# A pool of residual buffers with delayed reuse, and two norms moved into the next block, in a two-layer streaming encoder

## The chip, the cores and the metric

One Trainium2 chip, eight cores on two dies (cores 0 to 3 and 4 to 7). Every core runs the same program on two of the 16 sequences; there is no traffic between cores. The metric is the time of the slowest core in microseconds (us), lower is better. The program has two states: in some executions the cores of one die (at times both) are granted a lower TensorE clock, and the time is 1 to 19% longer.

## The reference, cut to what matters

```python
def reference(x, ...):                      # x: (16, 2048, 1024) float32
    h = x
    for layer in range(2):
        h = h + 0.5 * swiglu(rms_norm(h, ffn1_norm[layer]), ...)
        hn = rms_norm(h, mix_norm[layer])
        if layer == 0: h = h + chunked_relpos_attention(hn, ...)   # 16 heads, band of 9 chunks
        else:          h = h + mla_attention(hn, ..., shared k, v) # 8 heads, block-causal
        h = h + 0.5 * swiglu(rms_norm(h, ffn2_norm[layer]), ...)
        if layer == 0: k_nope, k_rope, v = mla_shared_kv(rms_norm(h, kv_norm), ...)
    return rms_norm(h, final_norm)
```

The residual stream `h` of a core (two sequences of 2048 tokens, 1024 channels, float32, 16 MB) does not stay on the core. Each block reads it from HBM, adds its result, and writes it to HBM again.

## The kernel before

The blocks run in the order F00 F01 A0 A1 F10 F11 F20 F21 B0 B1 F30 F31 (F feed-forward, A and B attention; the last digit is the sequence). In each block, TensorE works through 32 output pieces of 128 channels x 512 tokens. A piece ends in one VectorE add: PSUM bank plus residual piece. `Resid` brings the residual piece (256 KB) in, and takes the sum out. All these transfers are issued by SyncE from one queue, in program order:

```python
class Resid:
    def __init__(self, src, srcR, dst, dstR, order, more=(), n_rr=4):
        self.ring = [(r[:], rR, 'r%d' % k) for k, (r, rR) in enumerate(rr[:n_rr])] + list(more)
        ...
    def ahead(self, n=None):                       # issue loads for pieces < n
        n = len(self.ring) - 1 if n is None else n
        while self.n < min(n, len(self.order)):
            i, sb = self.order[self.n]
            r, rR, ch = self.ring[self.n % len(self.ring)]
            dma(r, xview(src, i, sb), [srcR[sb][i]], [rR], ch + 'l')
            self.n += 1
    def add(self, i, sb, po, poR, scale):
        ...
        TT(r, po, r, ALU.add, [poR, rR], [rR])     # bank + residual, in place
        dma(xview(dst, i, sb), r, [rR], [dstR[sb][i]], ch + 's')
        self.ahead(n + len(self.ring))             # loads piece n+9 into the buffer of piece n-1
```

The ring has 10 buffers in A (four `rr`, six in the arena), 7 in B, 4 in F. While a block ends, the norms of the next block run beside it: `norm_plan` spreads, over the projections, per 512-token slice a 2 MB load (`load`), squares on ScalarE (`sq`), a sum over channels on TensorE and the reciprocal root (`st`), and eight VectorE multiplies into `hn` (`nrm`).

```python
# a_block, head: 8 projections before the first scores, on two PSUM banks (MISC_A = [6, 7])
fill = [g for a in range(8) for g in proj(a)]
for _ in range(8):
    fill.pop(0)()
...
# a_block, at the start of the last head pair
if a == 7 and bl == 0:
    more = [...arena buffers at 84, 86, 2, 6, 12, 14 K...]
    rs = Resid(src, srcR, dst, dstR, [(i, t0 + s) for s in range(4) for i in range(8)], more)
    rs.ahead()
    wo = wo_groups('a', ao, aoR, rs, t0)           # 32 output projections of 8 matmuls
```

The softmax here doesn't subtract the row's maximum and nothing guards it: scores larger than these inputs give would overflow.

## Time and profile before

| | before |
|---|---|
| two runs before the prediction | 5358.67 (fast) and 6034.01 (slow), median 5696.34 us |
| profiled run (slow state) | cores 0 to 3: 5328 to 5345 us; cores 4 to 7: 5507 to 5530 us |
| TensorE busy, page of the slowest core | 97% |
| TensorE waits on core 0 | 135 us |

The page's first two sections show a kernel with one full engine. What is left to gain can only be found by asking where that engine stands still:

```profile
PE 5380.4 (97%) x29888; PEld 2603.0 (47%) x29888; DVE 1948.6 (35%) x3083; ACT 1533.0 (28%) x2068; POOL 231.9 (4%) x681
PE   8999999999899999999999999999998999999999
```

Slices of 10 us of core 0 at the end of A0 show the place in one look. The columns are window, length, TensorE busy, granted clock, DMA share, GB/s:

```profile
1300.00:1310.00 10.00, 7.84 (x37) 1.00 0.97 211
1310.00:1320.00 10.00, 0.00 (x0) 0.55 1.03 184
1320.00:1330.00 10.00, 6.29 (x16) 0.60 0.73 227
```

TensorE does nothing for one slice, and its clock falls in that slice and stays low in the next. The names in such lines: `ps` is a PSUM bank; `xs` is the residual stream in HBM; `arena`, `rr`, `sg` and `hn` are buffers on the core; `wbf<-wblob` is the load of a weight tile; SPq is the queue that SyncE issues from. In a line of waits, such as those in the prediction, the three numbers are total us, count and longest us. In a line of the order of time, the bracket is the idle time ahead of the group and what ended it.

### The profile page before, as it was taken

Reading aid. Unit: us, or ns where it says so; the run is one execution under the profiler, and the core shown is the slowest. Engines: PE = TensorE matmul, PEld = TensorE weight load, DVE = VectorE, ACT = ScalarE, POOL = GpSimd, SP = SyncE. Lnnn points to the kernel's source line nnn. Section 1 sums busy time; section 2 is a strip of 40 time slices with the busy share of each in tenths; the row PEclk is TensorE's granted clock in tenths of the full one; section 3 lists DMA queues with packets and bytes.
Section 4 is the critical chain, followed back from the end, with each engine's and each line's share of the span. In section 5 each row is a group of like instructions: output and inputs, shape, how many; then the busy total and the mean of one; then the engine's idle time right before and its main releaser. Section 6 shows DMA issues by size and latency. Waiting matters only on the chain.

```text
span 5530.0 us, 80374 instructions; the slowest of 8 cores (5328.5 to 5530.0 us)
## 1 busy us (share of the span) xinstructions
PE 5380.4 (97%) x29888; PEld 2603.0 (47%) x29888; DVE 1948.6 (35%) x3083; ACT 1533.0 (28%) x2068; POOL 231.9 (4%) x681
## 2 busy tenths in 40 slices
PE   8999999999899999999999999999998999999999
PEld 3444444455455444444444444445654664444445
DVE  2113111346566412321531351143444443133312
ACT  3111111147467412111211211113443442121311
POOL 0000000000010000000000000000000000000000
PEclk7888888899999999999999999999999999999999
DMA  5125312522522622632642363263264255255442
GB/s 132 31 37 146 95 31 35 150 68 68 148 54 70 189 51 51 169 77 41 150 125 39 73 166 75 42 161 85 62 166 107 62 155 137 39 128 151 107 86 92
DMA packets 237403, 532.20 MB, mean 96 GB/s; under 512 B 21472, under 2 KB 30176, under 8 KB 237024
## 3 DMA queue, kind: packets, MB, share of 16 engines
q1 hardware_dynamic: 194544, 356.11, 20.8%
q0 software_dynamic: 42480, 170.97, 18.5%
q8 instruction: 247, 4.05, 0.3%
q14 instruction: 132, 1.08, 0.1%
HBM read 577.88 MB, written 111.67 MB: 125 GB/s over the span
## 4 chain that ended last, share of the span: by engine, by line
PE 90%; DMA 5%; DVE 2%; issue 1%; ACT 1%; SPq 0%; DVEq 0%; POOL 0%; ACTq 0%; POOLq 0%
PE ps L407 90%; DMA xs<-rr 2%; DMA xs<-arena 1%; DVE hn L418 1%; DVE arena L424 1%; DVE arena L414 1%; ACT arena L411 0%; ACT rstd L411 0%; DMA rr<-xs 0%; DMA xn<-xT 0%; PE ps L1476 0%; SPq L404 0%; DMA arena<-xs 0%; ACT L411 0%; DMA xn<-tabT 0%
## 5 line engine op out<-in xcount | busy, mean ns | idle before, releaser
L407 PE MATMUL ps<-hn,wbf 128*128 128x512 bf16 (+1 forms) x13280 | 3050.9, 392 | 43.2 <-DVE arena L414 30.4
L407 PEld LDWEIGHTS ps<-hn,wbf 128*128 128x128 bf16 x13280 | 1324.2, 100 | 1683.0 <-issue 504.5
L407 PE MATMUL ps<-arena,wbf 128*128 128x512 bf16 (+1 forms) x6520 | 1481.5, 388 | 11.7 <-DVE rr L414 5.5
L414 DVE TENSOR_TENSOR arena<-sg,ps 128x512 bf16<-128x512 f32 (+1 forms) x706 | 483.9, 686 | 1961.5 <-PE ps L407 1910.5
L407 PEld LDWEIGHTS ps<-arena,wbf 128*128 128x128 bf16 x6520 | 648.7, 100 | 796.1 <-issue 220.3
L411 ACT ACTIVATE sg<-ps 128x512 f32<-128x512 f32 (+1 forms) x706 | 420.6, 596 | 1990.9 <-PE ps L407 1971.7
L411 ACT ACTIVATE arena<-ps 128x1024 bf16<-128x1024 f32 (+2 forms) x520 | 484.7, 975 | 465.6 <-PE ps L407 429.0
L407 PE MATMUL ps<-arena 64*128 64x256 bf16 (+8 forms) x5728 | 567.8, 264 | 28.9 <-DVE arena L414 6.4
L407 PEld LDWEIGHTS ps<-arena 128*128 128x128 bf16 (+1 forms) x5728 | 348.8, 96 | 253.6 <-issue 174.3
L411 ACT ACTIVATE sq<-xn 128x1024 f32<-128x1024 f32 (+3 forms) x264 | 243.5, 949 | 530.6 <-DVE sq L414 267.4
L418 DVE SCALAR_TENSOR_TENSOR rr<-ps,rr 128x512 f32<-128x512 f32 x224 | 154.9, 691 | 649.2 <-PE ps L407 633.7
L424 DVE CAST arena<-ps 128x512 bf16<-128x512 f32 x368 | 252.0, 689 | 259.6 <-PE ps L407 259.1
L456 POOL DMA_DIRECT2D wbf<-wblob x290 | 153.2, 528 | 4054.9 <-PE ps L407 4003.9
L418 DVE SCALAR_TENSOR_TENSOR hn<-xn,gains_sb,rstd 128x512 bf16<-128x512 f32 (+1 forms) x440 | 295.4, 736 | 62.1 <-ACT rstd L411 62.1
L411 ACT ACT_TABLE_LOAD x45 | 57.7, 1283 | 381.7 <-PE ps L407 380.0
L414 DVE TENSOR_TENSOR sq<-sq 128x1024 f32<-128x1024 f32 (+1 forms) x128 | 139.0, 1086 | 36.6 <-ACT sq L411 33.3
L407 PE MATMUL ps<-wbf,hn 128*128 128x128 bf16 x2048 | 124.9, 219 | 3.0 <-DVE arena L424 3.0
L407 PEld LDWEIGHTS ps<-wbf,hn 128*128 128x128 bf16 x2048 | 118.3, 98 | 17.8 <-issue 8.3
L424 DVE COPY arena<-ps 128x512 f32<-128x512 f32 (+1 forms) x192 | 109.5, 598 | 43.7 <-PE ps L1476 36.2
L414 DVE TENSOR_TENSOR arena<-arena 128x512 bf16<-128x512 bf16 (+1 forms) x304 | 106.6, 372 | 35.8 <-ACT arena L411 27.2
L411 ACT ACTIVATE rstd<-ps,eps_sb 128x512 f32<-128x512 f32 (+1 forms) x74 | 50.0, 676 | 237.0 <-PE ps L407 236.8
L407 PE MATMUL ps<-sq,ones_sb 128*128 128x512 bf16 (+1 forms) x276 | 74.6, 400 | 40.0 <-ACT sq L411 23.3
(51 smaller groups left out, 1254.3 us busy)
## 6 DMA issues: line engine op xcount, KB each, us to landing
wbf<-wblob POOLq DMA_DIRECT2D x192, 512.0 KB, 5.3
xn<-xs SPq DMA_DIRECT2D x48, 2048.0 KB, 13.9
xs<-rr SPq DMA_DIRECT2D x282, 256.0 KB, 3.8
rr<-xs SPq DMA_DIRECT2D x218, 256.0 KB, 4.7
wbf<-wblob POOLq DMA_DIRECT2D x60, 704.0 KB, 7.2
arena<-xs SPq DMA_DIRECT2D x70, 256.0 KB, 4.5
xs<-arena SPq DMA_DIRECT2D x70, 256.0 KB, 4.7
wbf<-wblob POOLq DMA_DIRECT2D x22, 768.0 KB, 7.8
```

The source lines that it names most:

```text
L407: sch.add('pe', lambda e: e.matmul(out, lhsT, rhs, start=start, stop=stop, skip_group_check=skip), rd, wr)
L411: sch.add('act', lambda e: e.activation(out, in_, func, **kw), rd, wr, None, [out], srcs)
L414: sch.add('dve', lambda e: e.tensor_tensor(out, a, b, op), rd, wr, None, [out], [a, b])
L418: sch.add('dve', lambda e: e.scalar_tensor_tensor(out, a, sc, b, op0, op1), rd, wr, None, [out], srcs)
L424: sch.add(eng, lambda e: e.tensor_copy(out, in_), rd, wr, None, [out], [in_])
L456: sch.add('pool', lambda e, wb=wb, w=w, src=src: e.dma_start(out=wb[:, 0:w], in_=src), rd, [wbR], 'wq%d' % k)
```

## The change

The intent is to keep TensorE fed where one block ends and the next begins. The ring becomes a pool of free buffers, in which a buffer is offered again only `cool` adds after its own; more buffers join the pool in A and B; two of A1's four norms move from A0's tail into A1's start; and A's first projections use six PSUM banks.

```diff
+LATE_A = [('A', 0, 1)]
 class Resid:
-            def __init__(self, src, srcR, dst, dstR, order, more=(), n_rr=4):
+            def __init__(self, src, srcR, dst, dstR, order, more=(), n_rr=4, cool=3):
+                self.cool = cool
+                self.hot = []
-                self.ring = [...] + list(more)
+                self.free = list(more) + [(r[:], rR, 'r%d' % k, 99) for k, (r, rR) in enumerate(rr[:n_rr])]
+            def ahead(self):
+                while self.n < len(self.order):
+                    self.free = [f for f in self.free if f[3] >= self.n]   # 'last piece' of a buffer
+                    if not self.free: break
+                    slot = self.used[(i, sb)] = self.free.pop(0)
+                    ...load...
             def add(...):
                 ...add, store...
-                self.ahead(n + len(self.ring))
+                self.hot.append(slot)
+                if len(self.hot) > self.cool:
+                    self.free.append(self.hot.pop(0))
+                self.ahead()
 # feed-forward blocks
+            rs = Resid(..., cool=1)
 # A, last head pair
+                    more = f32_slots(ar, [o_ * K for o_ in (2, 6, 12, 14)], 'rc')
+                    more += [(r[:], rR, 'rs%d' % k, 27) for k, (r, rR) in enumerate(sg)]
+                    more += f32_slots(ar, [84 * K, 86 * K], 'ra')
+                if a == 7 and bl == 2:
+                    free_s = [s for s in (1, 2) if next_jobs[s].fine]
+                    rs.more(f32_slots(hn_ar, [...four per slice in free_s...], 'rh', 23))
 # A, head
+            if late_a: fill[9:15] = fill[12:15] + fill[9:12]
+            cur['misc'] = MISC_E                    # six banks
+            for n in range(8):
+                if late_a and n == 0: jobs[2].st()
+                elif late_a and n == 6: jobs[3].st()
                 fill.pop(0)()
+                if late_a and n < 4: jobs[2].nrm(n); jobs[3].sq(n)
+            cur['misc'] = MISC_A
 # B: three hn buffers more where the next block is F30, and later up to nine more
# [cut: norm_plan(n_full=2) for A1, jobs[3].nrm among A1's first groups, B's pool in full, bookkeeping]
```

More of the change, by code (lines that the diff above doesn't have):

```diff
@@ L618, in nrm, with hn @@
                         ALU.mult, ALU.mult, [self.xR, rsR, gR], [self.hR[0][c] if self.fine else self.oR])
+            def hn(self, c):
+                return self.hR[0][c] if self.fine else self.oR
             def store(self):
@@ L678, in kfin, with norm_plan @@
                     self.xR.rd.extend(r.rd)
-        def norm_plan(jobs, pitch, lag=1, base=0):
+        def norm_plan(jobs, pitch, lag=1, base=0, n_full=4):
             plan = {}
@@ L689, in norm_plan @@
                 kv, final = j.a[4], j.a[5]
-                for q in range(4):
-                    put(b - 4 + q, j.sq, q)
+                if n <= n_full:
+                    for q in range(4):
+                        put(b - 4 + q, j.sq, q)
+                if n >= n_full:
+                    continue
                 put(b, j.st)
@@ L732, in next_plan @@
         def next_plan(blk, next_jobs, par):
-            if BLOCKS[BLOCKS.index(blk) + 1] in LATE:
+            nb = BLOCKS[BLOCKS.index(blk) + 1]
+            if nb in LATE:
                 for n in range(1, 4):
@@ L736, in next_plan @@
                 return late_plan(next_jobs, *par[1])
+            if nb in LATE_A:
+                for n in range(2, 4):
+                    next_jobs[n].fine = True
+                plan = norm_plan(next_jobs, *par[0], n_full=2)
+                return plan
             return norm_plan(next_jobs if blk[0] == 'A' else next_jobs[::-1], *par[0])
         class Resid:
-            def __init__(self, src, srcR, dst, dstR, order, more=(), n_rr=4):
+            def __init__(self, src, srcR, dst, dstR, order, more=(), n_rr=4, cool=3):
+                self.cool = cool
+                self.hot = []
                 self.a = (src, srcR, dst, dstR)
@@ L744, in __init__, with more @@
                 self.n = 0
-                self.ring = [(r[:], rR, 'r%d' % k) for k, (r, rR) in enumerate(rr[:n_rr])] + list(more)
-                self.first = 0
-                self.slots = {}
-            def ahead(self, n=None):
+                self.free = list(more) + [(r[:], rR, 'r%d' % k, 99) for k, (r, rR) in enumerate(rr[:n_rr])]
+                self.used = {}
+            def ahead(self):
                 src, srcR = self.a[:2]
-                n = len(self.ring) - 1 if n is None else n
-                while self.n < min(n, len(self.order)):
+                while self.n < len(self.order):
+                    self.free = [f for f in self.free if f[3] >= self.n]
+                    if not self.free:
+                        break
                     i, sb = self.order[self.n]
-                    r, rR, ch = self.ring[self.n % len(self.ring)]
+                    slot = self.used[(i, sb)] = self.free.pop(0)
+                    r, rR, ch, _ = slot
                     dma(r, xview(src, i, sb), [srcR[sb][i]], [rR], ch + 'l')
                     self.n += 1
+            def more(self, slots):
+                self.free += slots
+                self.ahead()
             def add(self, i, sb, po, poR, scale):
                 dst, dstR = self.a[2:]
-                n = self.order.index((i, sb))
-                r, rR, ch = self.ring[n % len(self.ring)]
+                slot = self.used.pop((i, sb))
+                r, rR, ch, _ = slot
                 if scale == 1.0:
@@ L766, in add, with f32_slots @@
                 dma(xview(dst, i, sb), r, [rR], [dstR[sb][i]], ch + 's')
-                self.ahead(n + len(self.ring))
+                self.hot.append(slot)
+                if len(self.hot) > self.cool:
+                    self.free.append(self.hot.pop(0))
+                self.ahead()
+        def f32_slots(arena, offs, name, last=99):
+            out = []
+            for n, o in enumerate(offs):
+                a_, r_ = arena.take(o, 1024)
+                out.append((a_.bitcast(F32), r_, '%s%d' % (name, n), last))
+            return out
         def ffn_block(blk, jobs, src, srcR, dst, dstR, bg_up, next_jobs, last):
@@ L843, in ffn_block @@
                 late_norms(1)
-            rs = Resid(src, srcR, dst, dstR, [(i, t0 + s) for i in range(8) for s in range(4)])
+            rs = Resid(src, srcR, dst, dstR, [(i, t0 + s) for i in range(8) for s in range(4)], cool=1)
             kv = blk in KV_IN
@@ L1018, in proj @@
                 out = []
+                gv_ = {}
                 for s in range(4):
@@ L1027, in gqk @@
                         w3, wR = w3_()
-                        pp, ppR = misc(MISC_A)
+                        pp, ppR = misc(cur['misc'])
                         for c in range(8):
-                            MM(pp, w3[:, c, o:o + 128], job.o3[:, c, :], c == 0, c == 7, [wR, job.oR], [ppR])
+                            MM(pp, w3[:, c, o:o + 128], job.o3[:, c, :], c == 0, c == 7, [wR, job.hn(c)], [ppR])
                         CP(dst_[0], pp, [ppR], [dst_[1]])
@@ L1034, in gv @@
                         w3, wR = w3_()
-                        pp, ppR = misc(MISC_A)
+                        pp, ppR = misc(cur['misc'])
                         for tt in range(4):
@@ L1038, in gv @@
                                 MM(pp[:, tt * 128:(tt + 1) * 128], job.o3[:, c, tt * 128:(tt + 1) * 128],
-                                   w3[:, c, 256:384], c == 0, c == 7, [wR, job.oR], [ppR])
+                                   w3[:, c, 256:384], c == 0, c == 7, [wR, job.hn(c)], [ppR])
                         CP(v_out(v_[s][0]), pp.rearrange('p (t h n) -> p t h n', t=4, h=2), [ppR], [v_[s][1]])
@@ L1042, in gv, with done @@
                             w_done(('a', 'qkv', a))
-                    out += [lambda s=s, g=gqk: g(0, q_[s]), lambda s=s, g=gqk: g(128, k_[s]), gv]
+                    def done(s=s):
+                        gv_[s]()
+                        made.add((a, s))
+                    gv_[s] = gv
+                    out += [lambda s=s, g=gqk: g(0, q_[s]), lambda s=s, g=gqk: g(128, k_[s]), done]
                 return out
@@ L1068, in scores @@
                 a, QB, rs_, first, last = groups[g]
-                assert len(fill) <= 3 * (31 - 4 * a - QB) or a == 7, (a, QB, len(fill))
+                assert (a, QB) in made, (a, QB)
                 q_, k_, v_ = bufs[a % 2]
@@ L1140, in a_block @@
             bias_load(0)
+            late_a = blk in LATE_A
+            made = set()
             fill = [g for a in range(8) for g in proj(a)]
-            for _ in range(8):
+            if late_a:
+                fill[9:15] = fill[12:15] + fill[9:12]
+            cur['misc'] = MISC_E
+            for n in range(8):
+                if late_a and n == 0:
+                    jobs[2].st()
+                elif late_a and n == 6:
+                    jobs[3].st()
                 fill.pop(0)()
+                if late_a and n < 4:
+                    jobs[2].nrm(n)
+                    jobs[3].sq(n)
+            cur['misc'] = MISC_A
             bias_make(0)
@@ L1156, in a_block @@
             shape(1)
+            if late_a:
+                jobs[3].nrm(0)
             for b in range(NB):
@@ L1166, in a_block @@
                 if a == 7 and bl == 0:
-                    more = []
-                    for i, o in enumerate((84 * K, 86 * K, 2 * K, 6 * K, 12 * K, 14 * K)):
-                        a_, r_ = ar.take(o, 1024)
-                        more.append((a_.bitcast(F32), r_, 'ra%d' % i))
+                    more = f32_slots(ar, [o_ * K for o_ in (2, 6, 12, 14)], 'rc')
+                    more += [(r[:], rR, 'rs%d' % k, 27) for k, (r, rR) in enumerate(sg)]
+                    more += f32_slots(ar, [84 * K, 86 * K], 'ra')
                     rs = Resid(src, srcR, dst, dstR, [(i, t0 + s) for s in range(4) for i in range(8)], more)
@@ L1173, in a_block @@
                     wo = wo_groups('a', ao, aoR, rs, t0)
+                if a == 7 and bl == 2:
+                    assert len(fill) <= 3
+                    free_s = [s for s in (1, 2) if next_jobs[s].fine]
+                    rs.more(f32_slots(hn_ar, [s * 4096 + o_ * 1024 for s in free_s for o_ in range(4)], 'rh', 23))
                 if a == 6:
@@ L1197, in a_block @@
                     shape(2 * b + 3)
+                if late_a and b < 3:
+                    jobs[3].nrm(b + 1)
                 while done < n_fill and fill:
@@ L1242, in kv_home @@
                         v_.rearrange('p (h t n) -> p h t n', h=2, t=4), vR, vo)
-            kvh = [[kv_home() for _ in range(2 if s < 2 else 1)] for s in range(4)]
+            kvh = []
+            for s in range(4):
+                o_kv3 = o
+                kvh.append([kv_home() for _ in range(2 if s < 2 else 1)])
             qh = []
             for s in range(4):
+                o_q3 = o
                 q_, qR = tk(1024)
@@ L1552, in b_block @@
             rs = wo = None
+            got = False
             def do_fill():
@@ L1570, in b_block @@
                 if p == 3 and bl == 0:
-                    more = []
-                    for i in range(4):
-                        a_, r_ = ar.take(o_ckv + i * 1024, 1024)
-                        more.append((a_.bitcast(F32), r_, 'rb%d' % i))
+                    more = f32_slots(ar, [o_ckv + i * 1024 for i in range(4)], 'rb', 27)
+                    if next_jobs[3].fine:
+                        more += f32_slots(hn_ar, [3 * 4096 + i * 1024 for i in range(3)], 'rh', 27)
                     rs = Resid(src, srcR, dst, dstR, [(i, t0 + s) for s in (3, 2, 1, 0) for i in range(8)], more, 3)
@@ L1577, in b_block @@
                     wo = wo_groups('b', ao, aoR, rs, t0, 0)
+                if p == 3 and bl == 8:
+                    assert seen['p'] >= last_unit(3, lambda u: u[1] >= 6)
+                    more = f32_slots(ar, [o_kv3, o_kv3 + 1024, o_q3], 'rk')
+                    if next_jobs[2].fine:
+                        more += f32_slots(hn_ar, [2 * 4096 + i * 1024 for i in range(3)], 'rg', 23)
+                    rs.more(more)
+                if p == 3 and not got and (3, 0) in made:
+                    got = True
+                    end = 99 if seq == 0 else 27
+                    rs.more([(r[:], rR, 'rs%d' % k, end) for k, (r, rR) in enumerate(sg)]
+                            + [(rr[3][0][:], rr[3][1], 'r3', end)])
                 if p == 2 and next_jobs:
```

## The prediction

> **What bounds the kernel now.** I read the list of cores first, because the two times on record (5358.67 and 6034.01 us) are two states of one program, then the page's busy shares, then TensorE's waits, then TensorE and the DMA-issuing queue around the few places where TensorE stands still.
>
> ```profile
> core 0: 5340.0 us, clock 0.990
> core 1: 5345.0 us, clock 0.992
> die 0 (median of its cores): 5341.6 us, clock 0.992
> die 1 (median of its cores): 5516.9 us, clock 0.957
> ```
>
> The page is of a core of the slow die. I work on core 0, of the undisturbed one, and predict the fast state, whose one run took 5358.67 us. The windows of core 0, added up, give PE 5192 us busy in 5345 us: 153 us, 2.9%, is all the idleness there is, and everything that the change does must come out of it. TensorE's waits on core 0, the largest:
>
> ```profile
> PE ps L407 <- DVE arena L414: 44.7, 31, 14.7
> PE ps L407 <- DVE rr L414: 22.9, 7, 11.8
> PE ps L407 <- ACT sq L411: 17.9, 11, 7.9
> ```
>
> L414 is VectorE's add or multiply; with out tile rr or arena it is above all the residual add that empties a PSUM bank of an output projection. Asked by stretch, the waits of the eight feed-forward blocks are almost nil (none at all from 90 to 960 us). The long ones stand at four seams, where an attention block ends: A0 to A1 (about 1308 us), A1 to F10 (1679), B0 to B1 (3977), B1 to F30 (4383). The order-of-time view of TensorE there:
>
> ```profile
> 1295.59 12.25 PE L407 MATMUL ps<-arena,wbf 128*128 128x512 bf16 x56
> 1322.52 6.29 PE L407 MATMUL ps<-hn,wbf 128*128 128x512 bf16 x16 [14.68 <-DVE arena L414]
> 1330.81 3.08 PE L407 MATMUL ps<-wbf,hn 128*128 128x128 bf16 x32 [1.99 <-DVE arena L424]
> ...
> 1690.66 3.57 PE L407 MATMUL ps<-sq,ones_sb 128*128 128x512 bf16 x8 [11.84 <-DVE rr L414]
> ...
> 3978.80 1.89 PE L407 MATMUL ps<-hn,wbf 128*128 128x512 bf16 x8 [1.45 <-DMA wbf<-wblob]
> 3991.97 14.81 PE L407 MATMUL ps<-hn,wbf 128*128 128x512 bf16 x56 [11.29 <-DVE arena L414]
> ...
> 4391.45 3.57 PE L407 MATMUL ps<-hn,wbf 128*128 128x512 bf16 x8 [6.57 <-DVE arena L414]
> 4400.95 3.57 PE L407 MATMUL ps<-sq,ones_sb 128*128 128x512 bf16 x8 [5.92 <-DVE rr L414]
> ```
>
> The first matmul of the next block needs a bank that an unfinished residual add still holds. VectorE in turn waits for data: from 1285 to 1332 us its waits are 21.9 us for arena<-xs and 5.3 us for rr<-xs, the loads of old residual pieces. And those loads are late because of the queue that issues them. From 1270 to 1332 us its waits are these two lines, and its order of time shows one load behind one store:
>
> ```profile
> SPq L152 <- DMA xs<-arena: 20.7, 7, 11.7
> SPq L152 <- DMA xs<-rr: 19.5, 4, 9.2
> ```
> ```profile
> 1300.89 0.74 SPq L404 DMA_DIRECT2D xs<-rr  x1
> 1313.36 0.32 SPq L404 DMA_DIRECT2D arena<-xs  x1
> 1313.78 0.58 SPq L404 DMA_DIRECT2D xs<-rr  x1
> 1323.60 0.32 SPq L404 DMA_DIRECT2D rr<-xs  x1
> ```
>
> So the chain is: store of piece n-1 lands, then the load of piece n+9 into its buffer can be issued, then the queue is free for the next store. TensorE makes a piece in 8 matmuls, 1.73 us; the queue needs a landing, 4.6 or 4.7 us in the median for these stores, up to 12 us late in the tail. Ten buffers (seven in B) are a lead that some 20 fast pieces use up.
>
> **What the Trainium skill says.** "DMA: Bandwidth & Descriptors", section "Anatomy of one DMA": any semaphore wait happens on the issuing sequencer before dispatch, and the completion receipt dominates the fixed cost. The trace agrees: 40.2 us of the queue's time in the two lines above are waits for stores. "TensorE: Matmul & The Clock Gate", section "Part 1: The HAM clock gate": after an idle window of about 3.4 us TensorE runs at half its clock until it has been busy for a window. The trace agrees: after 14.68 us of idleness 16 matmuls took 6.29 us against 3.62 us for such a group when warm. So each seam costs more than its wait. "HBM Reference", section "Specifications (TRN2)": about 358 GB/s per core when the pair is active. From 1185 to 1345 us the hardware queue moved 19.93 MB in 39.5% of 160 us, some 315 GB/s while busy, and no slice stayed above about 400; I use this as the limit that a faster tail could meet.
>
> **The change part by part.**
> (1) The residual ring becomes a pool of free buffers. A buffer is offered again only three further adds after its own (`cool=3`), so a load waits for a store issued 3 pieces, some 5.2 us, before, and usually landed. Up to three more stores are in flight. That removes the serial store-load chain. No transfer is added or dropped.
> (2) The pool is larger: in A 12 at once (six arena, four rr, two sg) plus 4 unused hn slots before A1 and 8 before F10, against 10; in B up to 13 before B1 and 19 before F30, against 7. In A0 piece 28 is loaded after add 19, nine pieces or 15 us ahead; in A1 the last load follows add 14.
> (3) In the F blocks the pool has the same four buffers and `cool=1`. A piece there takes 22 matmuls, 4.76 us, about a store's landing, and TensorE waits for nothing there: zero.
> (4) A1 starts with two of its four norms undone. The same 2 sums (8 matmuls, 1.73 us each) and 16 multiplies of 0.736 us move from A0's tail to A1's start: no gain in itself, but four hn slots for (2).
> (5) A's first projections rotate over six PSUM banks, not two: the 1.99 us wait above goes.
>
> What each seam costs, idle time plus the slow matmuls after it (warm groups: 8 in 1.89 us, 16 in 3.62, 32 short ones in 1.95, 56 in 12.25; 48 some 10.5, from 144 in 31.24):
> - A0 to A1: 14.68 + 1.99 + (6.29 - 3.62) + (3.08 - 1.95) + 0.56 (a group of 16 in 4.18) = 21.0 us.
> - A1 to F10: 11.84 + (3.57 - 1.89) + 1.3 (48 in 11.81) = 14.8 us.
> - B0 to B1: 11.29 + 1.45 + (14.81 - 12.25) = 15.3 us.
> - B1 to F30: 0.79 + 6.57 + 5.92 + 2 x 1.68 + 1.25 (48 in 11.75) = 17.9 us.
>
> Sum 69.0 us, 1.3% of 5358.67. What I leave standing: the weight tile of the next block. Its load is issued when six projections (10.4 us) are left and took 11.6 to 11.7 us in the median in these tails, so 1.5 us at A0 to A1 and 1.5 to 2.3 at B0 to B1; about 1 us at each F seam; some 1.5 us at A1's third slice, whose norm (sum 1.73, two activations 1.35, eight multiplies 5.9 us between six copies of 0.69) is ready only about when six projections (10.4 us) are through. And 2 us for the fourth norm among A1's first groups: VectorE is 22.45 us busy in 36 there, and 5.9 more fit, but unevenly. Together 9 us. Gain 69 - 9 = 60 us: 5358.67 - 60 = 5299 us.
>
> **The rivals.**
> (a) The DMA engines become the bound. The 160 us stretch holds 39.5% + 15.4% = 88 us of engine time at full rate, 74 us of it (61.1% + 19.9% of 92) between 1240 and 1332. With 7 more loads (1.8 MB, an estimated 6 us at 315 GB/s) moved ahead of 1240, and stores and weights (13 us) left after the seam, 55 us stand in 68: possible, but bursts can delay loads. Then half the gain stays, about 5325 us. For it: shares of 0.97 to 1.03 at 1300 to 1320. Against: early in the tail the share is far lower while the queue sits blocked.
> (b) New reuse waits: the next block writes into buffers whose last stores are in flight (A1's q, k, v of slices 2 and 3; weight issues on the pool queue behind memsets). If 5 us come back at each of four seams: 5319 us.
> (c) The small waits inside the tails (1 to 2 us each, some 10 us in all) go too, as VectorE loses norms from A0's tail, and nothing of the 9 us stands: 5285 us.
> (d) The idle time was thermally useful and the slow state becomes more frequent. That would change the state, not the fast time.
>
> **Range and chances.** The ceiling for the four seams is 69 us (1.3%), with the small waits about 80 us (1.5%); 2% would be 107 us, of 153 us of idleness that includes the start of the program and its end, which nothing touches. Hence faster by over 2% only 0.03. To be slower by 2% it would have to add a new stall larger than all seams together: 0.02. Within 2%: 0.95. Predicted 5299 us, and 5275 to 5335 eight times in ten: the low end is rival (c) with 0.2% of run noise, the high end rival (a) with the same.
>
> **What would show it.** Right: on a fast core, the four waits of 6 to 15 us are gone from TensorE's list, and the clock in these stretches is 1.00; the queue's waits for xs<-rr and xs<-arena fall from some 40 us to under 10 in A0's tail; VectorE no longer waits for arena<-xs; the wait for wbf<-wblob is a little larger; feed-forward blocks are unchanged. Rival (a) shows as loads that are issued early and land late; (b) as VectorE or GpSimd waiting for DMA xs<-arena at a block's start. I would be wrong if idle time elsewhere, such as within A's groups, moved by tens of us, or if the projections of A1 starved on late norms.

## The result, and the profile after

Ratios are the mean time of one kernel's fast runs over that of the other's of the same rounds, so not quite the ratio of the medians.

| | before | after |
|---|---|---|
| runs in this comparison, of them slow | 11, 7 | 12, 4 |
| fast runs, mean | 5357.3 us | 5290.7 us |
| ratio of fast runs | | 0.9876 (0.9862 to 0.9889) |
| median of all runs | 5733.85 us | 5291.92 us |

The change is 1.2% faster, inside the 2% that separate "same" from "faster". The medians of all runs differ by 8%, but only because more of the runs of the kernel before fell in the slow state; nothing here shows that this is the kernel's doing, and it is not explained.

The list of cores of the kernel after, whose profiled run was fast:

```profile
core 0: 5276.4 us, clock 0.996
die 0 (median of its cores): 5281.1 us, clock 0.996
die 1 (median of its cores): 5282.1 us, clock 0.996
```

TensorE's waits on core 0 after, the lines of the same releasers (line numbers have moved by one):

```profile
PE ps L408 <- ACT sq L412: 17.6, 10, 8.1
PE ps L408 <- DVE arena L415: 12.2, 30, 2.1
PE ps L408 <- DVE rr L415: 1.9, 2, 1.0
PE ps L408 <- DMA wbf<-wblob: 1.7, 2, 0.9
```

The wait for arena adds falls from 44.7 to 12.2 us, and its longest from 14.7 to 2.1; that for rr adds from 22.9 to 1.9. The first line, of which some 10 us belong to the program's start, is as it was. Of SyncE's queue from 1270 to 1332 us, where the prediction shows 20.7 and 19.5 us of waits for stores, this is what is left:

```profile
SPq L152 <- DMA xs<-arena: 4.4, 1, 4.4
```

The granted clock in the stretches of 28 to 34 us at the four seams (the places where an attention block ends) rose from 0.68, 0.76, 0.78 and 0.75 to 0.95 at A0 to A1 and 1.00 at the others.

TensorE in order of time, where A0 ends (1308 us), where A1 ends (1665), where B0 ends (3951), and where B1 ends (4352):

```profile
1306.65 1.89 PE L408 MATMUL ps<-sq,ones_sb 128*128 128x512 bf16 x8
1308.38 3.62 PE L408 MATMUL ps<-hn,wbf 128*128 128x512 bf16 x16
...
1327.19 0.58 PE L408 MATMUL ps<-arena 64*128 64x384 bf16 x3 [2.51 <-DVE arena L425]
...
1664.64 1.89 PE L408 MATMUL ps<-sq,ones_sb 128*128 128x512 bf16 x8
...
3950.93 8.79 PE L408 MATMUL ps<-hn,wbf 128*128 128x512 bf16 x40 [0.72 <-DMA wbf<-wblob]
...
4351.98 1.89 PE L408 MATMUL ps<-sq,ones_sb 128*128 128x512 bf16 x8
```

The first group of A1 starts without a wait, 16 matmuls in 3.62 us and not 6.29. What came in its place at A0 to A1 is the 2.51 us. It answers to a line of VectorE's own waits in that stretch:

```profile
DVE arena L425 <- DMA xs<-arena: 6.5, 1, 6.5
```

VectorE wants to copy A1's third q slice into an arena buffer from which one of the last four residual pieces is still being stored. In A1's, B0's and B1's tails VectorE waits for no DMA at all.

For time per seam I take the moments at which weight tiles are released (they show as GpSimd's issue of the next tile, the same sequence in both kernels), core 0:

| seam | before | after | saved | forecast |
|---|---|---|---|---|
| A0 to A1 (980.36 to 1392.01; 982.74 to 1378.05) | 411.65 | 395.31 | 16.3 | 21.0 - 5.0 |
| A1 to F10 (1675.97 to 1731.77; 1661.95 to 1703.51) | 55.80 | 41.56 | 14.2 | 14.8 - 1 |
| B0 to B1 (3967.59 to 4107.16; 3935.28 to 4060.93) | 139.57 | 125.65 | 13.9 | 15.3 - 2 |
| B1 to F30 (4372.46 to 4442.07; 4326.30 to 4378.29) | 69.61 | 51.99 | 17.6 | 17.9 - 1 |

Together 62.1 of the 63.6 us by which core 0's span fell. Between the seams A1 and B1 took the same time to 0.1 us. The stretch from F10 through B0 moved by -8, -8, -4 and +4 us on cores 1, 2, 0 and 3, the part before A0's tail by -2.4 to +2.6; why is not known.

The forecast was made from core 0, and core 0 shows the most. By the same moments the four seams together saved 52.5, 53.0 and 52.0 us on cores 1, 2 and 3; B0 to B1 alone saved 8.7 to 9.6 there, against 13.9 on core 0. DMA traffic has the same bytes, but in A0's tail it is denser: the stores xs<-arena landed in 8.2 us in the median, against 4.6 before, the loads arena<-xs in 4.8 against 3.9, the weight tiles in 14.7 against 11.7.

### The profile page after: what moved, and what is told of

Its sections match the earlier page's. It is cut to its first block, busy times and chain, and to the rows that moved or that the text cites. A ratio compares the mean times of both kernels' runs of the same rounds, so it can differ in the third digit from the quotient of the medians.

```text
span 5286.4 us, 80454 instructions; the slowest of 8 cores (5271.3 to 5286.4 us)
## 1 busy us (share of the span) xinstructions
PE 5177.1 (98%) x29888; PEld 2555.8 (48%) x29888; DVE 1948.2 (37%) x3083; ACT 1533.1 (29%) x2068; POOL 231.9 (4%) x681
## 4 chain that ended last, share of the span: by engine, by line
PE 91%; DVE 3%; DMA 2%; issue 2%; ACT 1%; SPq 0%; DVEq 0%; POOL 0%; ACTq 0%; POOLq 0%
PE ps L408 91%; DVE hn L419 1%; DMA xs<-arena 1%; DVE arena L415 1%; DVE arena L425 1%; ACT arena L412 0%; DMA xs<-rr 0%; ACT rstd L412 0%; DMA xn<-xs 0%; DMA xn<-xT 0%; PE ps L1536 0%; DMA wbf<-wblob 0%; ACT L412 0%; DMA hn<-tabQ 0%; ACT sq L412 0%
## 5 line engine op out<-in xcount | busy, mean ns | idle before, releaser
L408 PE MATMUL ps<-hn,wbf 128*128 128x512 bf16 (+1 forms) x13280 | 2915.7, 379 | 22.5 <-DMA wbf<-wblob 6.4
L408 PEld LDWEIGHTS ps<-hn,wbf 128*128 128x128 bf16 x13280 | 1291.8, 98 | 1559.1 <-issue 51.4
L408 PE MATMUL ps<-arena,wbf 128*128 128x512 bf16 (+1 forms) x6520 | 1419.2, 376 | 11.1 <-DVE arena L415 4.0
L408 PEld LDWEIGHTS ps<-arena,wbf 128*128 128x128 bf16 x6520 | 634.3, 98 | 747.7 <-issue 17.7
L435 POOL MEMSET arena<- 64x128 bf16 (+2 forms) x348 | 69.3, 207 | 916.3 <-ACT arena L412 883.8
```

Source lines behind the costliest of these rows:

```text
L408: sch.add('pe', lambda e: e.matmul(out, lhsT, rhs, start=start, stop=stop, skip_group_check=skip), rd, wr)
L435: op = sch.add('pool', lambda e: e.memset(out, v), extra, wr)
```

## The experiments

Theory Q: the serial chain "store lands, then load is issued, then the next store" in the SyncE queue caused the late loads, and the delayed reuse breaks it. Rival P: the larger pool did it. Rival L: the late norms did. All kernels below gave correct results. "Unresolved" means that intervals overlap.

### Reuse at once: e1_cool0

```diff
-            def __init__(self, ..., n_rr=4, cool=3):
+            def __init__(self, ..., n_rr=4, cool=0):
```

> The changed kernel with one number undone: in A and B a buffer is offered again right after its own add (cool 0 in place of 3), so each load waits in the queue for the store that was issued just before it. The pool stays as large. Theory Q (the serial store-load chain in the issuing queue is the cause, and the delay of three adds is what breaks it): the queue falls behind by some 5 us for each of the 16 recycled pieces before A1, so a wait of 10 us or more comes back at A0 to A1, a smaller one at A1 to F10; the total is 20 to 40 us over the changed kernel, ratio to the kernel before 0.992 to 0.995. Rival P (the larger pool alone is the cause): same as the changed kernel, ratio 0.987 to 0.989, and no TensorE wait over 3 us at the seams.

One fast run of four, 5351.70 us, against 5349.4 us (mean of six) for the kernel before: all of the gain is gone, with the pool as large as in the changed kernel. The single run gives no interval, but the cores of undisturbed dies say the same, 5339.9 us (4 dies) against 5339.6 (13 dies), and the profile is clear. The queue's waits in A0's tail (core 0), and TensorE's group after it:

```profile
SPq L152 <- DMA xs<-arena: 58.1, 10, 24.5
```
```profile
1329.39 3.57 PE L408 MATMUL ps<-hn,wbf 128*128 128x512 bf16 x8 [21.29 <-DVE arena L415]
```

Waits of 11.0 and 7.5 us stood at B0 to B1 and one of 7.8 us after A1; B1 to F30, with 19 buffers, was clean. The direction is Q's, but the loss is larger than Q said. Nor is this the rule of the old ring: there a load waits for the store of the piece *before* the one just stored, which is `cool=1`. `cool=0` is worse than anything in either kernel, so this run doesn't isolate the pool. Run e9 does.

### Few buffers, delayed reuse: e2_few

```diff
-  more += [... sg ...];  free_s = [...];  B: + hn, rk, rg, sg, rr3
+  (A: rc, ra, rr = 10 buffers; B: rb, rr = 7, all usable to the end)
```

> The changed kernel with the old number of buffers (10 in A, 7 in B) but the delayed reuse (cool 3). Theory Q: nearly all of the gain stays; the lead is 6 pieces (10.4 us) in A and 4 pieces (6.9 us) in B against landings of 5 to 8 us, so at most 5 us come back at each seam in B; ratio 0.988 to 0.992. Rival P: the gain is lost for the most part, ratio 0.995 or more, with waits of 6 to 15 us at all four seams.

Ratio 0.9975 (0.9955 to 0.9995). My expectation (Q's) was wrong: most of the gain is gone, as P said. The queue's waits for stores from 1225 to 1345 us were 15.8 us (56.3 in the kernel before): the serial chain is largely broken. But now the loads themselves are too late, because buffers come back too late. VectorE's wait in B1's tail, and TensorE after it:

```profile
DVE arena L415 <- DMA arena<-xs: 26.2, 11, 9.8
```
```profile
4381.53 3.57 PE L408 MATMUL ps<-sq,ones_sb 128*128 128x512 bf16 x8 [11.26 <-DVE arena L415]
```

The last load there was issued at 4363.96 us; its add, waiting for that DMA, ran at 4381.92: some 18 us from issue to use. I had set the lead of 4 pieces (6.9 us) against landings of 5 to 8 us, the medians. TensorE's long wait here ended with a load far later than these, issued while four weight tiles (12.3 us each in the median) loaded beside it.

### Without the late norms: e3_no_late

```diff
-LATE_A = [('A', 0, 1)]
+LATE_A = []
```

> The changed kernel without the two late norms at the start of A1 (all four norms in A0's tail again, and no hn buffers in A0's pool). My theory: the late norms only move work, and 12 buffers with delayed reuse are enough: within 4 us of the changed kernel (ratio 0.987 to 0.989); the 2.5 us wait of TensorE for VectorE's copy near the start of A1 may go or stay. Rival L (the late norms are what opens the seam A0 to A1): a wait of 10 us or more comes back there, ratio 0.990 to 0.991.

Ratio 0.9895 (0.988 to 0.991), fast mean 5293.2 us: the changed kernel within the resolution. Rival L falls. The wait for VectorE's copy went, one of 4.06 us for the weight tile stood at A1's start on core 0.

### Two banks at A's start: e4_banks2

```diff
-            cur['misc'] = MISC_E
+            cur['misc'] = MISC_A
```

> The changed kernel with the first projections of A on two PSUM banks as before. My theory: the 1.99 us wait at the start of A1 comes back in some form, 1 to 4 us in all (copies and late norms alternate on VectorE, 2.1 us per projection against 1.73 on TensorE), ratio 0.987 to 0.989, not resolved in the total but visible at the start of A1. Rival: two banks make the first projection wait for the last residual adds, 5 us or more.

Ratio 0.9891 (0.9871 to 0.991), unresolved from the changed kernel. Its profile fell in the slow state; on core 4, of the undisturbed die, the start of A1 had a wait of 1.25 us for the weight tile and one of 1.49 us for ScalarE, and no bank wait. With the adds in time, the six banks are not needed. My expected 1 to 4 us are not seen.

### The late norms and banks on the old ring: e5_old_ring

```diff
-        class Resid:  (pool)
+        class Resid:  (ring of the kernel before, 10 and 7 buffers)
```

> The late norms and the six banks at the start of A alone, with the old ring of buffers (the order of loads and stores as in the kernel before). Theory (the gain is in the residual traffic: both larger pool and delayed reuse are needed): no gain to speak of, ratio 0.996 to 1.000, waits of 6 to 15 us at all four seams; at A0 to A1 the wait moves to the sum of the late norm or a little later, as six banks let the projections begin. Rival (late norms and banks give a part of the gain by themselves): the seam A0 to A1 loses 8 us or more of its cost, ratio about 0.997 or lower.

Ratio 0.9997 (0.998 to 1.0014). Waits of 3 to 11 us stand at all four seams, at A0 to A1 split into 6.4, 4.3, 2.1 and 1.1 us. By themselves the late norms and banks give nothing.

### Reuse at once in the feed-forward blocks: e6_f_cool0

```diff
-            rs = Resid(..., cool=1)
+            rs = Resid(..., cool=0)
```

> The changed kernel with cool 0 in place of 1 in the feed-forward blocks only. Theory: a piece there takes 22 matmuls, 4.76 us, as long as a store takes to land, so the queue keeps up either way and TensorE waits for nothing: ratio as for the changed kernel, 0.987 to 0.990. Rival: with four buffers the load is issued only after the landing and comes late at the blocks where norm loads of 2 MB pass, waits of 2 us and more in feed-forward blocks, 5 us or more in all.

My expectation was wrong. The one fast run of six took 5384.04 us, some 90 us over the changed kernel, and the cores of undisturbed dies agree (5373.7 us, 6 dies). The profile was slow on both dies, so only waits that stand far out are read from it. TensorE's largest on core 6, which was 1.1 us there in the changed kernel:

```profile
PE ps L408 <- DVE sq L415: 47.9, 8, 8.1
```

The queue there waited 360.7 us for xs<-rr between 1750 and 3550 us (102.1 in the changed kernel). The 2 MB loads of the next block's norms are in the same queue behind those waits: ScalarE's squares waited 128.1 us for xn<-xs up to 3800 us (71.5 in the changed kernel), the sums came late, and the next matmul waited for them. These waits are about half of the loss; the rest is not traced. So a feed-forward block is not insensitive to the reuse rule; the change left it unharmed because `cool=1` is what the old ring did.

### Keeping the clock up: e7_warm

```diff
 # kernel before, start of A1
+            if seq == 1:
+                for _ in range(224):
+                    MM(P[5][0][:, 0:128], ones[:], ones[:], True, True, [onesR], [P[5][1]])
```

> The kernel before with 224 small extra matmuls (128 columns, some 56 ns each, 12.5 us in all, into a bank that nobody reads) at the start of A1, inside the 14.7 us that TensorE stands idle there. It measures the cost of the slow clock by itself. Theory (the groups after the wait are slow because TensorE stood idle): the groups of 16, 32 and 16 matmuls after the wait take 3.6, 1.95 and 3.6 us and not 6.3, 3.1 and 4.2, the seam gains 3 to 5 us, the total 0.1% at most (not resolved). Rival (they are slow for want of data or because of DMA traffic): they stay slow and the seam gains nothing.

Ratio 1.0006 (0.9986 to 1.0026). TensorE in order of time, core 0:

```profile
1310.44 12.67 PE L407 MATMUL ps<-ones_sb 128*128 128x128 bf16 x224
1322.95 3.62 PE L407 MATMUL ps<-hn,wbf 128*128 128x512 bf16 x16
1333.09 3.55 PE L407 MATMUL ps<-wbf,hn 128*128 128x128 bf16 x32 [6.52 <-DVE arena L424]
1336.45 3.63 PE L407 MATMUL ps<-hn,wbf 128*128 128x512 bf16 x16
```

The 16 matmuls took 3.62 us, not 6.29: the idleness was what had slowed them, as the Trainium skill's "TensorE: Matmul & The Clock Gate", section "Part 1: The HAM clock gate", says. The 32 short ones, which now follow an idle time of 6.52 us, were slow still (3.55 us). But the seam gained nothing. The next wait grew from 1.99 to 6.52 us, because the last residual adds still end when their loads land. From the end of A0's last 56 matmuls (1310.60) to the third group of A1 (1336.45) it is 25.9 us; in the kernel before, from 1307.84 to 1333.67, 25.8. By the release of weight tiles, as in the table above, the seam took 411.4 us against 411.7. The 2.67 us that the first slow group cost lay beside the lateness, they were not added to it; the slow groups after it were not tested by themselves. Both answers that I had offered were half right.

### Another order of the pool: e8_rr_first

```diff
+                    if next block is A1:
+                        rs.free = rs.free[8:] + rs.free[6:8] + rs.free[:6]   # rr, ra, rc, sg
```

> The changed kernel with the pool of A0 in another order (rr buffers first, then the arena buffers beyond A's working set, then the arena buffers that A1's first q, k and v go to, then sg), so that the last four pieces of A0 do not sit where A1 writes first. In the changed kernel VectorE waits 6.5 us for their stores, TensorE 2.5 us, and the clock falls for a moment. Theory: that wait goes, 3 to 5 us at the start of A1, ratio lower by 0.0005 to 0.001 than the changed kernel's: 0.9866 to 0.989. Rival: the wait moves to the late norms or to the weight tile and nothing is gained.

Ratio 0.9892 (0.9875 to 0.9908), unresolved. The wait of 2.51 us for VectorE is gone as meant, but the next one was there: ScalarE wants A1's first bias tile, which SyncE issues after A0's last stores (at 1313.77 us) and which ScalarE could use at 1332.53, 18.8 us later for 256 KB. On core 0, in ScalarE's waits and TensorE's order of time:

```profile
ACT arena L412 <- DMA arena<-biasA: 4.6, 1, 4.6
```
```profile
1334.49 0.28 PE L408 MATMUL ps<-arena 64*128 64x256 bf16 x2 [2.19 <-ACT arena L412]
```

The rival held in its sense: the wait moved, though to the bias tile, which it had not named.

### The pool alone, with the old delay: e9_cool1 and e14_cool1

```diff
-            def __init__(self, ..., n_rr=4, cool=3):
+            def __init__(self, ..., n_rr=4, cool=1):
```

> The changed kernel with cool 1 in A and B: the old delay (a load waits for the store of the piece before its own trigger, as in the old ring) with the new large pool. Cool 0 was harsher than the old ring, so this is the fair test of the pool alone. Theory T (pool and delay are both needed: pool alone leaves the serial queue, delay alone leaves too short a lead): between, 10 to 40 us over the changed kernel, ratio 0.989 to 0.995, the cost at A0 to A1 and B0 to B1, where 16 and 19 loads go through the serial queue, and little at A1 to F10 and B1 to F30. Rival P (with a large pool the delay doesn't matter, only cool 0 hurts): same as the changed kernel, 0.987 to 0.989.

Ratio 0.9905 (0.9883 to 0.9928), fast mean 5294.9 us. That is in T's range of ratios, near its lower edge and not far from P's: the large pool with the old delay has most of the gain. The one long wait left is where the theory put it, at A0 to A1, with 16 buffers and all recycled loads behind stores. The queue's waits there, from 1225 to 1345 us, show that the chain was not gone (with xs<-sg they make 35.8 us, against 56.3 in the kernel before and 11.3 in the changed one):

```profile
SPq L152 <- DMA xs<-arena: 26.1, 7, 9.7
SPq L152 <- DMA xs<-rr: 6.7, 3, 2.4
```

TensorE's wait after it:

```profile
1330.94 3.57 PE L408 MATMUL ps<-hn,wbf 128*128 128x512 bf16 x8 [9.14 <-DVE arena L415]
```

B0 to B1, which I had named too, was clean. The repeat was made on one chip with the changed kernel:

> The large pool with the old delay of one add again, to compare with the changed kernel of the same set. From the run before: 3 to 8 us slower than the changed kernel, nearly all of it at A0 to A1 (9 us of waiting for a late residual add), which makes the pool the part that carries the gain and the delay worth under a tenth of it. Rival: 15 us or more slower.

Fast means: 5296.9 us (two runs), the changed kernel 5287.2 (three). Over all cores of undisturbed dies (8 and 10 dies): 5287.3 and 5280.7 us. So the delay of three adds is worth some 7 to 10 us of the 60, more than the tenth that I had expected.

### A longer delay: e10_cool6

> The changed kernel with cool 6: the queue waits for no store, but every recycled load is issued three pieces (5 us) later than in the changed kernel. Theory T (what counts is issue time against landing time; loads late in a tail take up to some 16 us to land): B0 to B1, whose lead falls from 10 to 7 pieces, gets 3 to 10 us of waits back, A0 to A1 (13 to 10 pieces before the last four) 0 to 5 us; the seams with 19 and 20 buffers stay clean; ratio 0.988 to 0.991. Rival: 5 us don't matter, same as the changed kernel.

```diff
-            def __init__(self, ..., n_rr=4, cool=3):
+            def __init__(self, ..., n_rr=4, cool=6):
```

Ratio 0.9928 (0.9906 to 0.9951), fast mean 5307.2 us, some 12 us over `cool=1` on the same chip. The queue waits for almost no store (3.2 us in A0's tail), but recycled loads start later: waits of 5.6 us (and 3.3 us for the weight tile) at A0 to A1, 10.8 us at B0 to B1, none over 1 us where the pool has 19 or 20 buffers. That is the direction and the place that the theory of issue time against landing time gave; the sizes are a little over it (a ratio of 0.991 at most, waits of up to 5 and 10 us).

### Early bias tile: e11_bias and e13_bias

```diff
 # on top of the reordered pool: A0's last head pair, ahead of the residual loads
+                    if seq == 0:
+                        bias_load(0); carry['bt'] = (bt, btR)
                     rs.ahead()
 # A1's start
-            bias_load(0)
+            if seq == 0: bias_load(0)
```

> The kernel with the reordered pool (the run before this one of that kind) and A1's first bias tile (256 KB) loaded at the start of A0's last head pair, ahead of the residual loads, and not after A0's last store. In that run ScalarE waited 4.6 us for this tile, TensorE 2.8 us, and eight matmuls ran at half clock. Theory: these waits go and 3 to 5 us of A1's start are gained; ratio 0.9865 to 0.9885, 0.05 to 0.1% under the changed kernel, hardly resolved in the total. Rival: again the next wait takes their place, no gain in the span of A1's start.

Ratio 0.9886 (0.9857 to 0.9914), unresolved. Again, with the changed kernel on the same chip:

> The reordered pool with the early bias tile again, to compare with the changed kernel of the same set. Theory: 3 to 8 us faster than that (0.05 to 0.15%), from the start of A1. Rival: less than 2 us.

On core 0 the start of A1 has now no wait over 0.7 us:

```profile
PE ps L408 <- DMA wbf<-wblob: 0.6, 1, 0.6
PE ps L408 <- DVE arena L415: 0.3, 1, 0.3
PE ps L408 <- DVE arena L425: 0.2, 1, 0.2
```

The mean over cores of undisturbed dies is 5276.9 us (11 dies), the changed kernel's 5280.7 (10 dies): 3.8 us less, the lower edge of what was expected. The fast runs, which follow the slowest core, are 5287.4 and 5287.2 us, three each: no gain shown in the metric. It is at least no slower than the changed kernel.

### The changed kernel again: e12_changed

> The changed kernel itself once more, on one chip with the next two. If the term of 9 us left standing was too large: ratio 0.9865 to 0.9885 again, 65 us or more. If it is the kernel before that differs from set to set: ratio 0.9885 to 0.990, 53 to 61 us, which is the 60 us forecast.

Only one of the 11 runs of the kernel before in this set was fast (5347.57 us), so no interval is given. The cores of undisturbed dies (10 dies of each kernel) are the better measure: 5340.9 us before, 5280.7 us after, a difference of 60.2 us, ratio 0.9887. So the first comparison's 67 us held a slow-ish set of the kernel before (5357 us; it ran at 5346 to 5349 us in all later sets), and the gain is nearer to 60 us. Why the kernel before differed by 10 us between sets stays open.

## Why the prediction was right or wrong

**The step that failed: the base of the change.** The time itself was right: 5299 us lies 0.2% over the mean of the fast runs, 5275 to 5335 us holds it, and the largest chance was on "within 2%". What failed is what this time was a change from. The prediction said "I work on core 0, of the undisturbed one, and predict the fast state, whose one run took 5358.67 us". The time given for the kernel before was the median of two runs, one of each state, 5696.34 us; set against that, 5299 us reads as a gain of 7%, and the change gives no such gain: fast against fast it is 1.24%, or 1.13% by cores in the later set. (The medians of all runs differ by about as much, but by the number of slow runs in each set.) The working, which is from the fast state throughout, forecast 60/5358.67 = 1.1%. A prediction has to put its change, as a ratio, beside its time wherever the base is a mixture of states.

**The seams: right on core 0.** Four seams, each within 1 us of its forecast saving (the table above), 62.1 us for 60; on cores 1 to 3 they saved 52 to 53 us, so the closeness is in part that of the core chosen. Most signs named came true: the queue's waits for stores fell from 40.2 to 4.4 us, VectorE waits for no arena<-xs, the wait for wbf<-wblob rose from 1.5 to 1.7 us, and the clock is 1.00 at three of the four seams. The ceiling of 358 GB/s that rival (a) leaned on was no hard one: the kernel before moved 402 GB/s in one slice of 4 us.

**The step of the mechanism that failed: "That removes the serial store-load chain" as the first cause.** The prediction gave the two parts no shares, but it listed the delay (1) ahead of the pool (2), and the expectation of e2_few followed it: "nearly all of the gain stays". The runs showed the pool in its place. The four corners, each against the kernel before of its own set:

| | old delay (`cool=1` or ring) | `cool=3` |
|---|---|---|
| old number of buffers | 0.9997 (e5_old_ring) | 0.9975 (e2_few) |
| large pool | 0.9905 (e9_cool1) | 0.9876 and, by cores, 0.9887 |

By the cores of undisturbed dies, which scatter less, they are 0.2 us (e5_old_ring), 14.9 (e2_few), 52.8 (e9_cool1; 53.6 in e14_cool1) and 60.2 us (e12_changed) under the kernel before. The pool alone carries most of it, the delay alone a fifth to a quarter; together they give a little more than the pool. The chain in the queue was real, but breaking it was not needed for most of the gain: in e9_cool1 the queue still waited 35.8 us for stores. What ends a wait is whether a load is issued long enough before its add. With the large pool 13 to 20 of the 32 loads need no buffer to come back; then the queue may lag for the rest.

**The slow clock's cost, added to each wait: right in the sum, not as a cost of its own.** At A0 to A1 I added 4.4 us for slow groups. e7_warm took 2.67 us of them away and the seam gained nothing, since there this time lay beside the wait for the last adds. The sum came out right because the lateness of the adds went: from the end of A0's 56 matmuls to A1's third group it was 25.8 us in the kernel before, and the changed kernel works through the first two groups in 5.2 us (1308.38 to 1313.62); the difference of 20.6 us is the sum of the terms that the prediction had there (14.68 + 2.67 + 1.99 + 1.13).

**Feed-forward "zero": right, but not for the reason given.** The reason was that a piece takes 4.76 us there, about a store's landing. That is as true with `cool=0`, and e6_f_cool0 lost some 90 us by it. It is zero because `cool=1` is the old order.

**The six banks, 1.99 us: not confirmed.** e4_banks2 shows no bank wait without them; that wait had been for late adds too.

**What I left standing, 9 us:** about right in sum (62 of 69 us saved on core 0), not in kind. The weight tile cost 0.7 us at B0 to B1, where I had said 1.5 to 2.3; rival (b), a store in flight under the next block's first writes, was the 2.51 us at A0 to A1. Rival (a) was seen in part: in A0's tail the stores xs<-arena landed later by three quarters and the loads arena<-xs by a quarter. No add waited for a load; the 2.51 us wait stands behind such a store. Rival (c) did not come; the small waits inside the tails stand.

**Rival (d):** both kernels have slow runs in nearly all sets; the runs don't settle whether one has more.

## What to carry to other kernels

Where an engine waits at the end of a stage for transfers that pass through a few buffers, compare the time from issue to use in the worst moment of the stage (here some 18 us) with the lead that the buffers give, and not with the median landing (here 4 to 8 us); memory that lies idle at that moment can give that lead. A queue that issues in order should not meet a wait on something that it has only just started (e1_cool0), and one step of delay is a large part of that remedy, but each step takes lead away (e10_cool6). State a forecast as a ratio to a run of the same state.

## What the Trainium skill lacked or had wrong

- "TensorE: Matmul & The Clock Gate", section "Part 1: The HAM clock gate", says that with three or more cores of a die on dense matmuls the die is held at 13/16 of the clock while the load lasts, and to budget for that. Here all eight cores ran for 5.29 ms, with TensorE busy 98% of the time on the slowest core, at a mean granted clock of 0.995 to 0.997 in 8 of 12 runs. In the four slow runs the disturbed die had between 0.827 and 0.965, one die at a time. The lowest of any run, 0.811 (e4_banks2), is about 13/16, so the slow state may be that limit for a part of a run; no run here shows whether it is.
- The same page, section "Back-to-back issue gap", gives about 131 ns per matmul of 512 columns as sustained with weight loads, and calls 216 ns an isolated figure. Here 144 in a row, each with its weight load, took 31.24 us, 217 ns each.
- The pages give an access latency for HBM at high load, but none says how the landing of a whole transfer grows under load, which is what sizes a pool. "DMA: Bandwidth & Descriptors", section "Anatomy of one DMA", has a fixed cost of about 2 us for the GpSimd path. The runs show 256 KB stores at 3.2 us in the median in a quiet tail (e1_cool0, B1), 4.6 in the kernel before, 8.2 in the changed kernel's A0 tail, and 18.8 us from issue to use for one 256 KB load behind stores and weight tiles.
- No page says that a cold clock can cost nothing. In e7_warm it did, for the first slow group: TensorE waited again for the same late producer (2.67 us faster matmuls, 25.9 against 25.8 us to the third group).
